# The second FFN product of 18 inner tiles by Strassen's algorithm, two tiles at a time, with running sums in DRAM

## The chip, the core and the metric

The kernel runs on one core of a Trainium2 chip. TensorE (PE in the profile) multiplies, VectorE (DVE), ScalarE (ACT) and GpSimd (POOL) do the elementwise work, and SyncE (SP) issues most DMAs; some are issued from ACT's and POOL's queues. Each engine works through its own instructions in order and waits on semaphores for the others. The metric is the device time of one execution in microseconds, the median of several runs.

## What is computed

The reference is a trunk of two residual layers over 1024 tokens of width 1024: a gated DeltaNet layer, then a chunked softmax attention layer, and a gated ConvFFN after each. The change is in the ConvFFN alone:

```python
FFN_DIM = 2816
def conv_ffn(xn, w_up, conv_w, conv_b, w_down):
    h = causal_dwconv(xn @ w_up, conv_w) + conv_b
    gate, val = h[..., :FFN_DIM], h[..., FFN_DIM:]
    return (jax.nn.silu(gate) * val) @ w_down

for layer in range(DEPTH):          # DEPTH = 2
    ...
    h = h + conv_ffn(rmsnorm(h, f_norm[layer]), f_w_up[layer], f_conv[layer], f_conv_b[layer], f_w_down[layer])
return rmsnorm(h, final_norm)
```

All data are float32. The kernel splits every matmul operand into a high and a low float32r part and adds three products (high x high, high x low, low x high). `triple` in the code is one such set of three matmuls of 128 x 128 by 128 x 512.

## The kernel before

`ffn(layer, ...)` handles one ConvFFN. The 2816 inner channels are 22 tiles of 128 (`FP = 22`). For each tile j the *first product* gives gate and val before the convolution, already by a Strassen form: seven products `product(j, n)` of 12 matmuls, n in the order 1, 7, 6, 5, 2, 4, 3, in place of eight. Their operands come from `operand(j, n)`: a VectorE sum of weight blocks where one is needed, an ACT copy for the high part (`uh`), a POOL difference for the low part (`ul`). `after(j, n)` takes results out of PSUM, mostly on VectorE (`keep`, `vpre`, `gpre`). Then come the convolution's taps (`taps`: the first on ACT, the others on VectorE over gate and val), `silu` on ACT, `gated` on VectorE, and `hidden`, which splits the 128 x 1024 tile into `hidh` (ACT) and `hidl` (VectorE).

The *second product* takes the inner tiles 0 to 17 in nine groups of two (`NG = 9`). For a group g, `down(g, u)` computes one of eight 128 x 1024 output tiles `pd` with 12 matmuls: four triples over two inner tiles and two token halves. In layer 0 outputs lie as features by tokens with the weights stationary, in layer 1 as tokens by features with the channels stationary. `down_sum` copies the result out of PSUM on ACT (`hr`) and adds it to the running sum `d_hu[u]` in DRAM by an accumulating DMA from POOL's queue; in group 0 it is written plainly from SP. In layer 0, group 0, the residual is loaded and added on VectorE; in layer 1 it comes in by transposes on PE in the steps where g = u. The last four inner tiles (18 to 21) are multiplied at the layer's end (`part`, `tile_of`), added to what is loaded back from `d_hu`, and handed on.

The order of all of this is written out by hand. `seq` lists PE's steps; a step is one `product`, one `down` or one part of the end. `at(i, f, rank)` puts other work into a list that is issued just before PE's step i, by rank. Work given at step i is not held until PE gets there: an engine goes on with its own instructions, and only a semaphore (a PSUM result, a free buffer, a landed DMA) stops it. `operand(j, n)` is given two steps ahead of its product, `after(j, n)` one step behind. From tile 3 on, a group's period is 14 products of two inner tiles and the eight `down` steps of an earlier group, placed by the offsets `offs`.

Memory is tight: all eight PSUM banks are used, four for the first product (`u`) and four for the second (`d`, two tiles of two banks), and rooms of SBUF are reused by tag. The rooms `h1_0` to `h1_7` (layer 1: `h2_0` to `h2_7`) hold the residual at the layer's start; later `hid` of three tiles in turn lies in 0 to 5, `hr` in 6 and 7.

## Time and profile before

| | |
|---|---|
| median of 3 runs | 2642.46 us (2642.02 to 2642.86) |
| profiled execution | 2643.1 us, its span 2641.4 us, granted clock 0.996 |
| PE busy | 2552.0 us, 14149 matmuls |
| VectorE, ACT, POOL busy | 1575.1, 1309.9, 1256.3 us |
| DMA moved | 303.62 MB, of it 69.21 MB on POOL's queue |
| first FFN product on PE, first to last matmul | layer 0: 681.2 to 1311.5 us; layer 1: 1946.6 to 2589.7 us |

The page of the profile gives busy times of the engines, the span in 40 slices, the DMA queues, the chain of work that ended last, the costliest groups of instructions (line, engine, operation, tiles out<-in, shape, count; then busy time, the mean of one, and the idle time before them with what ended it), and the DMA issues. Other views of the trace give the same for a stretch of time, and instructions in order of time. A stretch of 59.84 us is one period of the inner groups.

### The profile page before, as it was taken

The numbers are of one execution on the slowest core, as the hardware profiler recorded it, in microseconds if no ns is written. First come the engines' busy times: TensorE is split into PE (matmuls) and PEld (weight loads), VectorE is DVE, ScalarE is ACT, GpSimd is POOL, SyncE is SP. The second block draws the span as 40 slices with busy tenths as digits, with TensorE's granted clock in tenths as the row PEclk, the third lists the DMA queues.
The fourth block names the chain that finished last, engine by engine and source line by source line (L and its number), as shares of the span: only waits on it lengthen the run. The fifth ranks groups of instructions, "written<-read, shape, count | busy, mean of one in ns | idle before, by whom it ended". The sixth has DMA issues, their size and how long they took to land.

```text
span 2641.4 us, 39047 instructions
## 1 busy us (share of the span) xinstructions
PE 2552.0 (97%) x14149; PEld 2112.8 (80%) x14149; DVE 1575.1 (60%) x2840; ACT 1309.9 (50%) x2526; POOL 1256.3 (48%) x1330
## 2 busy tenths in 40 slices
PE   7999899999999999999999999998989999999998
PEld 5878788888778888888878788887877888888886
DVE  5755764554685555555676666666478455455556
ACT  5444456564444444444455555555345444444443
POOL 3655544345345555555535444443343455555551
PEclk9999999999999999999999999999999999999999
DMA  4434435555346666666631111114232566666654
GB/s 128 138 99 121 120 108 154 158 164 161 86 145 140 120 120 136 120 124 120 150 117 51 43 57 45 47 46 144 89 95 76 128 144 129 127 128 126 144 105 148
DMA packets 312017, 303.62 MB, mean 115 GB/s; under 512 B 32528, under 2 KB 245264, under 8 KB 311824
## 3 DMA queue, kind: packets, MB, share of 16 engines
q1 hardware_dynamic: 287856, 223.26, 28.4%
q0 software_dynamic: 19072, 69.21, 16.3%
q10 hardware_dynamic: 4896, 8.65, 0.9%
q8 instruction: 111, 1.82, 0.3%
q14 instruction: 82, 0.67, 0.1%
HBM read 183.04 MB, written 118.03 MB: 114 GB/s over the span
## 4 chain that ended last, share of the span: by engine, by line
PE 70%; DVE 8%; issue 4%; POOL 3%; DMA 2%; ACT 2%; SPq 0%; DVEq 0%; ACTq 0%; POOLq 0%
PE pu L1387 9%; PE pu L1385 9%; PE pu L1386 9%; PE acc L120 4%; PE acc L121 4%; PE acc L122 4%; PE pd L1689 2%; PE pd L1690 2%; PE pd L1688 2%; PE pd L1385 2%; PE pd L1387 2%; PE pd L1386 2%; PE acco L120 2%; PE acco L122 2%; PE acco L121 2%
## 5 line engine op out<-in xcount | busy, mean ns | idle before, releaser
L1355 POOL TENSOR_TENSOR ul<-r,uh 128x512 fp32r<-128x512 f32 x282 | 412.8, 1508 | 327.7 <-ACT uh L1373 320.2
L120 PE MATMUL acc<-xh,whi 128*128 128x512 f32 x896 | 375.2, 419 | 0.2 <-ACT xh L1094 0.2
L121 PE MATMUL acc<-xl,whi 128*128 128x512 f32 x896 | 353.7, 395 | 1.6 <-POOL xl L379 1.0
L122 PE MATMUL acc<-xh,wlo 128*128 128x512 f32 x896 | 352.9, 394 | 0.6 <-POOL wlo L105 0.6
L105 POOL TENSOR_TENSOR wlo<-wraw,whi 128x256 fp32r<-128x256 f32 (+1 forms) x293 | 235.6, 833 | 200.4 <-ACT whi L103 161.6
L1701 ACT COPY hr<-pd 128x1024 f32<-128x1024 f32 x128 | 129.9, 1015 | 311.3 <-PE pd L1690 152.6
L1373 ACT CAST uh<-r 128x512 fp32r<-128x512 f32 x296 | 180.7, 620 | 181.6 <-DVE r L1355 118.9
L1702 POOL DMA_DIRECT2D d_hu<-hr x128 | 112.1, 876 | 240.3 <-ACT hr L1701 231.2
L1387 PE MATMUL pu<-xh,ul 128*128 128x512 f32 x552 | 215.5, 390 | 5.1 <-POOL ul L1355 5.1
L1385 PE MATMUL pu<-xh,uh 128*128 128x512 f32 x552 | 215.4, 390 | 2.5 <-ACT uh L1373 1.0
L1386 PE MATMUL pu<-xl,uh 128*128 128x512 f32 x552 | 215.2, 390 | 1.0 <-POOL xl L379 1.0
L122 PEld LDWEIGHTS acc<-xh,wlo 128*128 128x128 f32 x896 | 168.9, 189 | 38.3 <-POOL wlo L105 1.0
L121 PEld LDWEIGHTS acc<-xl,whi 128*128 128x128 f32 x896 | 170.2, 190 | 25.7 <-POOL xl L379 3.1
L120 PEld LDWEIGHTS acc<-xh,whi 128*128 128x128 f32 x896 | 169.8, 190 | 22.9 <-ACT xh L1094 1.0
L1468 DVE SCALAR_TENSOR_TENSOR val<-vpre,colt,val 128x1023 f32<-128x1023 f32 (+2 forms) x92 | 115.5, 1255 | 108.8 <-ACT val L1465 108.7
L1355 DVE TENSOR_TENSOR r<-r,r 128x512 f32<-128x512 f32 x168 | 140.6, 837 | 41.6 <-POOL ul L1355 41.5
L1995 POOL TENSOR_SCALAR sS<-sS,st 128x640 f32<-128x640 f32 (+4 forms) x128 | 87.5, 687 | 141.9 <-DVE st L1994 125.2
L1355 POOL TENSOR_TENSOR dl<-dr,dh 128x512 fp32r<-128x512 f32 x72 | 121.8, 1692 | 53.8 <-ACT dh L1373 53.8
L1468 DVE SCALAR_TENSOR_TENSOR gate<-gpre,colt,gate 128x1023 f32<-128x1023 f32 (+2 forms) x92 | 145.7, 1584 | 0.3
L1355 DVE TENSOR_TENSOR keep<-pu,keep 128x512 f32<-128x512 f32 x84 | 58.0, 690 | 143.5 <-PE pu L1387 142.0
L1355 DVE TENSOR_TENSOR vpre<-pu,keep 128x512 f32<-128x512 f32 x84 | 57.7, 687 | 133.9 <-PE pu L1387 133.7
L1355 DVE TENSOR_TENSOR hidl<-val,hidh 128x1024 fp32r<-128x1024 f32 (+1 forms) x46 | 87.3, 1898 | 72.3 <-ACT hidh L1483 72.3
(376 smaller groups left out, 6820.1 us busy)
## 6 DMA issues: line engine op xcount, KB each, us to landing
d_hu<-hr POOLq DMA_DIRECT2D x128, 512.0 KB, 5.5
r<-in_f_w_up_dram SPq DMA_DIRECT2D x168, 256.0 KB, 4.9
dr<-in_f_w_down_dram SPq DMA_DIRECT2D x72, 256.0 KB, 5.2
wraw<-in_a_w_in_dram SPq DMA_DIRECT2D x32, 512.0 KB, 4.7
wraw<-in_a_w_out_dram SPq DMA_DIRECT2D x16, 512.0 KB, 3.8
d_r<-h ACTq DMA_DIRECT2D x32, 256.0 KB, 3.9
d_hu<-hr SPq DMA_DIRECT2D x16, 512.0 KB, 3.0
wraw<-in_w_kv_dram SPq DMA_DIRECT2D x16, 512.0 KB, 3.9
```

Of the source, the lines that this page charges most:

```text
L105: nc.gpsimd.tensor_tensor(lo[:, c], raw[:, c], hi[:, c].bitcast(F32), op=ALU.subtract)
L120: mm(ps, hi[:, kw, wcol : wcol + P], rh[k][s], start=st, stop=False)
L121: mm(ps, hi[:, kw, wcol : wcol + P], rl[k][s], start=False, stop=False)
L122: mm(ps, lo[:, kw, wcol : wcol + P], rh[k][s], start=False, stop=sp)
L1355: tt = lambda eng, o, a, b, op: eng.tensor_tensor(o, a, b, op=op)
L1373: copy(hi, src)
L1385: mm(ps, w[0][:, cw], x[0], start=first, stop=False, skip_group_check=True)
L1386: mm(ps, w[0][:, cw], x[1], start=False, stop=False, skip_group_check=True)
L1387: mm(ps, w[1][:, cw], x[0], start=False, stop=last, skip_group_check=True)
L1468: nc.vector.scalar_tensor_tensor(t_[:, a:c1], p_[:, a - step : c1 - step], w[:, 2 - step : 3 - step], t_[:, a:c1], op0=ALU.mult, op1=ALU.add)
L1701: nc.scalar.copy(hr, dps[g, u])
L1702: nc.gpsimd.dma_start(out=d_hu[u], in_=hr, accum_op=add)
```

## The change

The second product of the nine groups goes by Strassen's algorithm too (the form with 7 products). For two inner tiles, weights are four blocks a11, a12, a21, a22 (output half, inner tile) of 128 x 512 and channels four blocks b11 to b22 (inner tile, token half). `second(g, n)` is one of seven products of four triples, in the order 1, 2, 5, 3, 6, 7, 4, placed after every second product of the first FFN product (group 0: some after one). Its operands are prepared three steps ahead: `weights` (VectorE sums, ACT copy `dh`, POOL difference `dl`) and `channels` (sums on VectorE in place in `val`, ACT copy `eh`, difference `el` on POOL for n = 3, 6, 7, else on VectorE). `hidden` is gone for tiles 0 to 17.

Products 1 and 2 share a PSUM bank pair, 5 and 3 share one, and 6, 7 and 4 share one. `drain` takes the state out after each product: on ACT for n = 1, 2, 5, 3, 4; on VectorE for 6 and 7, which are added to what 3 and 5 left in SBUF. `send` then adds five of the seven (not 5 and 3), each as two transfers of 512 KB, to five running sums in DRAM by accumulating DMAs from POOL's queue: the first, E, is common to three output quarters, the other four belong to the quarters. In layer 0 the quarters start as the residual (`d_r`, now kept by quarters); in layer 1 they start from plain writes of group 0, and the residual comes in by transposes in the end part (`load_r`). At a layer's end E is loaded back and sent on to three quarters (`load_e`, `send_e`).

Rooms change: `val` lies in `h_0` to `h_3` in turn, the staging tiles of `drain` and of E in `h_4` to `h_7`, and `hid` of tiles 18, 19, 20 in 6 and 7, 4 and 5, 2 and 3. Weight blocks have one buffer each (`a11` to `a22`, `ay`), and rings of two hold `d` and `e`.

```diff
-        RINGS = dict(u=3, d=4 if layer == 1 else 2)
+        RINGS = dict(u=3, d=2, e=2)
...
-                    conv_t[j, v] = tp.tile([P, SEQ], F32, name=("gate", "val")[v], tag=("gate", "val")[v])
+                if v == 0:
+                    conv_t[j, v] = tp.tile([P, SEQ], F32, name="gate", tag="gate")
+                else:
+                    conv_t[j, v] = hp.tile([P, SEQ], F32, name="val", tag=f"h{layer + 1}_{j % 4}")
...
+                    room_ = {18: 6, 19: 4, 20: 2}[j]
+                    hid[j] = [hp.tile([P, SEQ], F32R, name=f"hid{i}", tag=f"h{layer + 1}_{room_ + n}") for n, i in enumerate("hl")]
...
+        ORDER = 1, 2, 5, 3, 6, 7, 4
...
-                offs = [0, 2, 3, 5, 6, 8, 9, 11]
-                if layer == 0 and g < 2:
-                    offs = ([3, 4, 6, 7, 9, 10, 12, 13], [1, 3, 4, 6, 7, 9, 10, 12])[g]
-                elif g == 0:
-                    offs = [3, 4, 5, 6, 8, 9, 10, 11]
-                for u, o in enumerate(offs):
+                for n, o in zip(ORDER, (2, 3, 5, 6, 8, 9, 11) if g == 0 else (-2, 0, 2, 4, 6, 8, 10)):
                     if c == 7 * (2 * g + 1) + 6 + o:
-                        step(("d", g, u), lambda g=g, u=u: down(g, u))
+                        step(("d", g, n), lambda g=g, n=n: second(g, n))
...
-            when[j].append((nx(j, {3: 7, 5: 6}.get(j, 5) if layer == 0 else 5), (hidden,), 1.9))
+            if j >= 2 * NG:
+                when[j].append(({18: pos["d", NG - 1, 4] + 3, 19: pos["d", NG - 1, 4] + 7}.get(j, nx(j, 5)), (hidden,), 1.9))
...
+        def weights(g, n):
+            a = lambda q: araw[g, q]
+            if n == 5:
+                araw[g, 0] = wf.tile([P, HALF], F32, name="ay", tag="ay", bufs=1)
+                tt(nc.vector, a(0), a(21), a(22), add)
+            elif n == 3:
+                tt(nc.vector, a(0), a(0), a(11), sub)
+                tt(nc.vector, a(12), a(12), a(0), sub)
+            elif n == 7:
+                tt(nc.vector, a(21), a(11), a(21), sub)
+            aops[g, n] = cut(a({1: 11, 2: 12, 5: 0, 3: 12, 6: 0, 7: 21, 4: 22}[n]), "d")
+
+        def channels(g, n):
+            b11, b12, b21, b22 = [conv_t[2 * g + k, 1][:, hs(s)] for k in range(2) for s in range(2)]
+            if n == 5:
+                tt(nc.vector, b11, b12, b11, sub)
+            elif n == 6:
+                tt(nc.vector, b11, b22, b11, sub)
+            elif n == 7:
+                tt(nc.vector, b12, b22, b12, sub)
+            elif n == 4:
+                tt(nc.vector, b21, b21, b11, sub)
+            src = {1: b11, 2: b21, 5: b11, 3: b22, 6: b11, 7: b12, 4: b21}[n]
+            bops[g, n] = cut_high(src, "e")
+            cut_low(src, *bops[g, n], nc.gpsimd if n in (3, 6, 7) else nc.vector)
+
+        def second(g, n):
+            new = n in (1, 5, 6)
+            if new:
+                banks[g] = [pacc.tile([P, SEQ], F32, name="pd", tag="d", bufs=2) for _ in range(2)]
+            w_, x_ = (aops[g, n], bops[g, n]) if layer == 0 else (bops[g, n], aops[g, n])
             for f in range(4):
+                triple(banks[g][f // 2][:, hs(f % 2)], w_, x_, kc[f], new, True)
+
+        def drain(g, n):
+            for u in range(2):
+                ps = banks[g][u]
+                if n in (6, 7):
+                    t_ = stage[g, n, u] = stage[g, 3 if n == 6 else 5, u]
+                    tt(nc.vector, t_, ps, t_, add)
+                else:
+                    t_ = stage[g, n, u] = hp.tile([P, SEQ], F32, name="stage", tag=f"h{layer + 1}_{4 + u + (0 if n in (1, 5) else 2)}")
+                    nc.scalar.copy(t_, ps)
...
+        def send(g, n):
+            for u in range(2):
+                if g == 0 and (layer == 1 or n == 1):
+                    nc.sync.dma_start(out=total(n, u), in_=stage[g, n, u])
+                else:
+                    nc.gpsimd.dma_start(out=total(n, u), in_=stage[g, n, u], accum_op=add)
+
+        def load_e(u):
+            stage["e", u] = hp.tile([P, SEQ], F32, name="stage", tag=f"h{layer + 1}_{4 + u}")
+            nc.sync.dma_start(out=stage["e", u], in_=d_e[u])
+
+        def send_e(n):
+            for u in range(2):
+                nc.gpsimd.dma_start(out=total(n, u), in_=stage["e", u], accum_op=add)
...
+            for q, n in ((11, 7), (12, 3), (21, 7), (22, 4)):
+                at(b_[n] - 2, lambda g=g, q=q: load_a(g, q), 3 + q / 100)
+            for n in ORDER:
+                at(p_[n] - 3, lambda g=g, n=n: weights(g, n), 1.2)
+                at(p_[n] - 3, lambda g=g, n=n: channels(g, n), 1.4)
+                at(p_[n] + 1, lambda g=g, n=n: drain(g, n), 0)
+                if n not in (3, 5):
+                    at(p_[n] + 2, lambda g=g, n=n: send(g, n), 0.5)
+        fin_at = pos["d", NG - 1, 4]
+        for u in range(2):
+            at(pos["d", NG - 1, 7] + 3, lambda u=u: load_e(u), 3)
+        for n, i in ((6, 4), (7, 5), (4, 6)):
+            at(fin_at + i, lambda n=n: send_e(n), 0.5)
```

Here `b_` is the step of product n in the group before. The removed functions (`down`, `down_sum`, `load_dn`, `load_row`, `load_h`, `load_r` of the groups) and the changed addresses of the loads at a layer's end are left out.

More of the change, by code (lines that the diff above doesn't have):

```diff
@@ L497, in trunk_kernel @@
     ctx_h = ExitStack()
-    d_r0, d_r1 = [[dram.tile([P, SEQ], F32, name=f"d_r{i}_{k}") for k in range(KT)] for i in range(2)]
+    d_r0, d_r1 = [{(c, s, u): dram.tile([P, SEQ], F32, name=f"d_r{i}_{c}{s}{u}") for c in range(2) for s in range(2) for u in range(2)} for i in range(2)]
+    quarter = lambda d, m, s: d[m // 4, s, m % 4 // 2][:, hs(m % 2)]
     d_y = [[dram.tile([P, HALF], F32, name=f"d_y{k}_{s}") for s in range(2)] for k in range(KT)]
@@ L1355, in ffn @@
         tt = lambda eng, o, a, b, op: eng.tensor_tensor(o, a, b, op=op)
-        d_hu = [dram.tile([P, SEQ], F32, name=f"d_hu{layer}_{u}") for u in range(KT)]
+        d_c = d_r if layer == 0 else {x_: dram.tile([P, SEQ], F32, name=f"d_c{x_[0]}{x_[1]}{x_[2]}") for x_ in d_r}
+        d_e = [dram.tile([P, SEQ], F32, name=f"d_e{layer}_{u}") for u in range(2)]
         left, right = ExitStack(), ExitStack()
@@ L1692, in down_sum @@
-        def down_sum(g, u):
-            hr = hrs[g, u]
-            if g == 0 and layer == 0:
-                tt(nc.vector, hr, dps[g, u], hr, add)
-                nc.sync.dma_start(out=d_hu[u], in_=hr)
-            elif g == 0:
-                nc.scalar.copy(hr, dps[g, u])
-                nc.sync.dma_start(out=d_hu[u], in_=hr)
-            else:
-                nc.scalar.copy(hr, dps[g, u])
-                nc.gpsimd.dma_start(out=d_hu[u], in_=hr, accum_op=add)
-        past, free = [], 0
@@ L1802, in fin_h @@
                     for m in range(KT):
[L1803 removed]
+                        nc.sync.dma_start(out=fh[m][:, hs(s)], in_=quarter(d_c, m, s))
                 rooms = [x for _ in range(3) for x in ("uh", "ul")]
@@ L1819, in load_t, with load_r @@
                 for c in range(2):
-                    nc.sync.dma_start(out=fh[t][:, hs(c)], in_=d_hu[4 * c + t // 2][:, hs(t % 2)])
+                    nc.sync.dma_start(out=fh[t][:, hs(c)], in_=d_c[c, t // 4, t % 4 // 2][:, hs(t % 2)])
+            res = {}
+            def load_r(t):
+                for c in range(2):
+                    if t < 4:
+                        tag = ("eh", "el", "dh", "dl")[t % 2 * 2 + c]
+                        r_ = wf.tile([P, 4, P], F32, name="res", tag=tag, bufs=2)
+                    else:
+                        r_ = actp.tile([P, 4, P], F32, name="res", tag=f"x{'hl'[c]}{t}_1")
+                    for u in range(2):
+                        nc.sync.dma_start(out=r_[:, 2 * u : 2 * u + 2], in_=d_r[c, t // 4, u].rearrange("p (f t) -> p f t", f=2)[:, :, kc[t % 4]])
+                    res[t, c] = r_
             def tile_of(t, ks):
@@ L1830, in f @@
                     for c in range(2):
+                        if ks[0] == 0:
+                            for f in range(4):
+                                nc.tensor.matmul(fps[t][c][:, f * P : (f + 1) * P], res[t, c][:, f], ident, is_transpose=True, start=f == 0, stop=False, skip_group_check=True)
                         for k in ks:
```

100 lines of the change are left out of this document (25 added, 75 removed).

## The prediction, on record before the changed kernel was run

> **What bounds the kernel now.** I read the page's engine shares first, then the stretches of 59.84 us that one group of the second FFN product takes, then the groups of instructions, the order in time on VectorE and POOL, and last the DMA queues.
>
> ```profile
> span 2641.4 us, 39047 instructions
> PE 2552.0 (97%) x14149; PEld 2112.8 (80%) x14149; DVE 1575.1 (60%) x2840; ACT 1309.9 (50%) x2526; POOL 1256.3 (48%) x1330
> ```
>
> A busy PE is not yet a PE at its pace, so the stage matters. Next come two groups of layer 0: all instructions, then those of the second product (`pd`), then those of the first (`pu`).
>
> ```profile
> 881.00:940.84 59.84, 59.84 (x266) 49.57 (x265) 34.73 (x32) 28.56 (x38) 32.68 (x28) 1.00 0.66 128
> 940.84:1000.68 59.84, 59.84 (x266) 49.56 (x265) 32.27 (x31) 28.55 (x38) 32.61 (x27) 1.00 0.64 123
> ```
>
> ```profile
> 940.84:1000.68 59.84, 23.06 (x98) 18.02 (x97) 0.00 (x0) 8.12 (x8) 1.00 0.64 123
> ```
>
> ```profile
> 940.84:1000.68 59.84, 39.38 (x168) 31.54 (x168) 6.89 (x10) 2.32 (x4) 1.00 0.64 123
> ```
>
> The columns are PE, its weight load, VectorE, ACT and POOL, then the granted clock, DMA share and GB/s (the last two rows lack POOL). PE never stops at a granted clock of 1.00. A group is 14 products of 12 matmuls for the first FFN product and 8 tiles of 12 for the second, 264 in all (266 with those that cross an edge). So 59.84/266 = 0.225 us for each matmul, and 22 steps of 2.72 us. The mean of 389 ns in the groups is longer since matmuls overlap, and it is not the price. In this stage the time is the number of matmuls; the other engines stand at 32.3, 28.6 and 32.6 of 59.84.
>
> **The change, part by part.** The durations, of six groups of layer 0:
>
> ```profile
> L1355 POOL TENSOR_TENSOR ul<-r,uh 128x512 fp32r<-128x512 f32 x85 | 122.5, 1490 | 62.5 <-ACT uh L1373 62.5
> L1373 ACT CAST uh<-r 128x512 fp32r<-128x512 f32 x84 | 51.5, 620 | 48.0 <-DVE r L1355 32.1 <-issue 15.6
> L1701 ACT COPY hr<-pd 128x1024 f32<-128x1024 f32 x48 | 48.7, 1015 | 105.4 <-PE pd L1387 104.8
> L1702 POOL DMA_DIRECT2D d_hu<-hr x48 | 42.0, 874 | 78.5 <-ACT hr L1701 71.2 <-ACT uh L1373 7.1 <-issue 0.2
> L1355 DVE TENSOR_TENSOR val<-val,gate 128x1024 f32<-128x1024 f32 x12 | 22.8, 1898 | 0.0
> L1355 DVE TENSOR_TENSOR hidl<-val,hidh 128x1024 fp32r<-128x1024 f32 x12 | 21.7, 1806 | 19.7 <-ACT hidh L1483 19.7
> L1355 DVE TENSOR_TENSOR keep<-pu,keep 128x512 f32<-128x512 f32 x24 | 16.6, 692 | 43.5 <-PE pu L1387 43.1
> L1468 DVE SCALAR_TENSOR_TENSOR val<-vpre,colt,val 128x1023 f32<-128x1023 f32 x12 | 15.4, 1284 | 33.5 <-ACT val L1465 33.5
> L1483 ACT CAST hidh<-val 128x1024 fp32r<-128x1024 f32 x12 | 12.6, 1052 | 0.0
> ```
>
> How VectorE and POOL hold each other up, in order of time:
>
> ```profile
> 966.52 0.68 DVE L1355 TENSOR_TENSOR r<-r,r 128x512 f32<-128x512 f32 x1
> 967.12 1.28 DVE L1468 SCALAR_TENSOR_TENSOR val<-vpre,colt,val 128x1022 f32<-128x1022 f32 x1
> 969.58 0.69 DVE L1355 TENSOR_TENSOR r<-r,r 128x512 f32<-128x512 f32 x1 [1.18 <-POOL ul L1355]
> 970.19 2.31 DVE L1468 SCALAR_TENSOR_TENSOR gate<-gpre,colt,gate 128x1023 f32<-128x1023 f32 x1
> ...
> 974.69 1.27 DVE L1468 SCALAR_TENSOR_TENSOR gate<-gpre,colt,gate 128x1022 f32<-128x1022 f32 x1
> ```
>
> ```profile
> 970.11 1.31 POOL L1355 TENSOR_TENSOR dl<-dr,dh 128x512 fp32r<-128x512 f32 x1 [0.57 <-ACT dh L1373]
> ```
>
> *PE.* Seven products of 12 replace eight tiles of 12: 12 matmuls less in each of 9 groups of 2 layers, 216 x 0.225 = 48.6 us off the engine that sets the end. The period would be 59.84 - 2.70 = 57.1 us. The residual's 64 transposes in layer 1 move to the end, equal in number: nothing either way.
>
> *VectorE, per group.* Two `hidl` go (-3.6 us). Four sums of channels, four of weights and four `el` come, 512 wide, and four drains (n = 6, 7) of 1024 out of PSUM: 12 x 0.68 (the undisturbed `r<-r,r`) + 4 x 1.38 (two `keep`) = 13.7. So 32.3 + 10.1 = 42 of 57.1.
>
> *ACT.* Out go two `hidh`, four `dh` and eight drains (2.1 + 2.5 + 8.1), in come fourteen copies of 512 and ten drains (8.7 + 10.2): +6.2, 35 of 57.1.
>
> *POOL.* Four `dl` become seven, three `el` are new, and eight accumulating DMAs become ten: 6 x 1.49 + 2 x 0.87 = +10.7, 43 of 57.1.
>
> No engine is above PE by its sum. What decides is lateness: an operand is made two steps (5.44 us) ahead, by a VectorE sum, an ACT copy and a POOL difference (0.68 + 0.62 + 1.49 = 2.8). VectorE is gated by PE wherever it reads PSUM. Its fullest stretch goes from the drain of n = 6 to the next `keep`, five steps or 13.6 us. In it the new order has two drains (5.5), a `gpre`, two tile sums, a channel sum and an `el` (5 x 0.68), another tile sum (0.68) and four taps (5.1): 14.7 by the rows, but adjacent VectorE rows overlap by about 0.09 (966.52 + 0.68 against 967.12), so some 13.5. VectorE thus falls two to three us behind there, the 2.6 us of slack are used up, and it catches up in the next five steps, where it has some 6 us of work. POOL's fullest three steps hold four differences (6.0) of 8.2. I take 0.2 us of stall for each of 16 inner groups, +3; the ends are 0 and the rival on the interface below.
>
> *The interface that VectorE and POOL share.* The tap at 970.19 starts inside POOL's difference (970.11 to 971.42) and takes 2.31 instead of 1.27: it waits most of that difference. The Trainium skill, "SBUF — State Buffer", section "Who interferes with whom", says that a VectorE instruction with two SBUF inputs and a POOL instruction that reads SBUF exclude each other for the whole instruction. The trace agrees, by that 1.04 us. What it would make of the time is the third rival.
>
> *SP's and POOL's queues, inside the groups.* Loads of second-product weights stay four per group of 256 KB each; the eight residual loads and eight plain writes of layer 0's first group go. Each new load waits for the last reader of its only buffer, a difference of the step before, so SP stands up to 2 us; behind it are loads of up-weights that are needed more than five steps later: nothing. POOL's sends of n = 6 and 7 wait for VectorE's drain, and the next `ul` stands behind them; that is in the two to three us of lateness above.
>
> *The start of each layer.* Without `hidden` for tiles 0 to 2 the head gets lighter on VectorE, and group 0's operands, with one product instead of two between some of its seven, make it heavier. I take 0, with 3 us either way per layer.
>
> *The tail, where the DMAs come in.*
>
> ```profile
> q1 hardware_dynamic: 287856, 223.26, 28.4%
> q0 software_dynamic: 19072, 69.21, 16.3%
> ...
> d_hu<-hr POOLq DMA_DIRECT2D x128, 512.0 KB, 5.5
> r<-in_f_w_up_dram SPq DMA_DIRECT2D x168, 256.0 KB, 4.9
> ```
>
> An accumulating transfer of 512 KB lands 5.5 us after issue. Queue 0 spends 16.3% of 2641.4 us on 69.21 MB, 3.26 us of all sixteen engines for each 0.524 MB, so transfers issued close together land 3.26 apart. Inside a group that is covered: ten take 33 of 57 us, and a staging tile is written again only four or five steps (11 to 14 us) after its send. At a layer's end it is not. Put 0 at PE's start of the last product (n = 4, group 8). It ends at 2.7, ACT has drained it at 4.9, and POOL sends its two halves at 6.5 behind one `ul`. Then come six more, the first sum E added to three totals (`send_e`, indices +4 to +6). Eight transfers one behind another: the last lands at 6.5 + 5.5 + 7 x 3.26 = 34.8. Now `hidden(19)`, at index +7 (19.0 us), writes into the rooms `h_4` and `h_5` that E was staged in. ACT waits for the seventh, VectorE for the eighth, and all that is queued behind waits too: the difference ends at 36.6, a gate tap at 37.9, `keep` and `keep7` at 39.2. The last tile's product 4 adds onto the bank that `keep7` reads. It would start at index +10, 27.2, so PE stands 12 us, and about 1 more for product 3, whose sum is queued behind `gated`. `hidden(18)` waits likewise for its two sends, within the lead. SP waits for E's last accumulation before it loads E back, with the last tile's two loads behind it, needed five and more steps later; POOL's `ul` of products 7, 6 and 5 stand between the six sends and are ready by their step or an us late, inside the 12. That is 13 per layer, +26. The low end: if each lands 5.5 after its own issue (about 22 for the last) VectorE is through at 32, +9 for both layers. The high end: loads run ahead of them (0.88 us of queue 1 for each 256 KB, 28.4% of the span over 223.26 MB): eight last weight tiles, 7 us a layer, and in layer 1 sixteen residual pieces, 7 more, +47. I take the middle: most weight loads fall in gaps before.
>
> *Sum.* -48.6 + 3 + 0 + 26 = -19.6. The profiled execution took 2643.1, 0.6 above the median of 2642.46 of the three runs: 2643.1 - 19.6 = 2623.5, against the median 2623.
>
> **The rivals.** *The tail is hidden.* The sends keep pace and the inner groups lose nothing: -48.6 + 9 = 2603. For it: a single send lands in 5.5 with loads beside it. Against: six go out in about three steps, which this trace never has.
>
> *The tail eats it.* Loads in front, +47: -48.6 + 3 + 47, 2644, no change.
>
> *Slower: VectorE and POOL run out of their shared interface, in the inner groups.* Per group POOL has 24 differences of 1.31, VectorE 20 instructions of 0.68 and 10 of 1.28 with two SBUF inputs: 31.4 + 13.6 + 12.8 = 57.8 of 57.1, where before it was 18 x 1.31 + 8 x 0.68 + 12 x 1.28 = 44.4 of 59.84. If nothing overlaps, the interface and not PE sets the pace; filled to 95%, a group takes 60.8 and 18 of them lose 63 us against the forecast's 57.3: 2686. It decides from a period of 58.4 us, where 18 x 1.1 us use up the 19.6. Against it: a POOL row lasts 1.31 and the tap lost 1.04, so about 0.2 of each difference is free of it, 24 x 0.2 = 5 us per group, and some 53 of 57 remain. The page named above, whose rule holds the interface for the whole instruction, would make it this rival.
>
> That PE's count does not fall is no rival: the loops fix 84 for 96.
>
> **How the numbers follow.** Forecast 0.44 (2610 to 2637), tail hidden 0.18, tail eats it 0.14, interface 0.24. What a measurement can tell from no change is 0.2%, 5.3 us. Faster gets the forecast and the hidden tail, 0.62; same gets most of the third, 0.13; slower the interface and a rest, 0.25. The range of 8 in 10 goes from 2600 to 2664: from just below the hidden tail into the milder half of the interface case.
>
> **What would show it.** Right: windows of 57.1 us with about 254 matmuls and PE full; POOL near 43, VectorE 42 to 46 in them; ten accumulating sends per group; one PE gap of some 12 us per layer before the last tile's product 4, released by VectorE's `keep`, with ACT's `hidh` waiting for a DMA. Wrong: gaps in every group, with `ul` or `dl` as releaser and VectorE taps of over 2 us (third rival), or no such gap at the ends (first).

## The result: slower by 1.57%

| | median, us | range, us | ratio to before |
|---|---|---|---|
| before | 2642.24 (4 runs) | 2641.02 to 2642.86 | 1 |
| after | 2683.79 (4 runs) | 2680.91 to 2685.69 | 1.0157, 95% 1.0139 to 1.0175 |

The forecast was 2623, its range 2600 to 2664. The page of the changed kernel:

```profile
span 2683.3 us, 39404 instructions
...
PE 2542.1 (95%) x13933; PEld 2083.7 (78%) x13933; DVE 1807.4 (67%) x3084; ACT 1410.3 (53%) x2714; POOL 1492.2 (56%) x1490
```

PE has its 216 matmuls less (14149 to 13933), yet the span is 41.9 us longer. To find the places, I take two marks in each layer from the view of a tile's instructions: the product with `x7` (product 7 of the first FFN product, once per inner tile) and the product with `x` and `uh`, whose last start is nearly the end of the first product. Each row ends with its first and its last start. Before:

```profile
L1385 PE MATMUL pu<-x7h,uh x84: 389/389/497, 717.6 to 1296.2; 128*128 128x512 f32 x84
...
L1385 PE MATMUL pu<-xh,uh x276: 387/389/486, 681.2 to 1311.0; 128*128 128x512 f32 x138
...
L1385 PE MATMUL pu<-x7h,uh x84: 389/389/389, 1986.4 to 2571.1; 128*128 128x512 f32 x84
...
L1385 PE MATMUL pu<-xh,uh x276: 387/389/501, 1946.6 to 2589.3; 128*128 128x512 f32 x138
```

After:

```profile
L1389 PE MATMUL pu<-x7h,uh x84: 389/389/794, 728.1 to 1304.5; 128*128 128x512 f32 x84
...
L1389 PE MATMUL pu<-xh,uh x276: 387/389/794, 685.8 to 1329.4; 128*128 128x512 f32 x138
...
L1389 PE MATMUL pu<-x7h,uh x84: 389/389/793, 2019.3 to 2594.4; 128*128 128x512 f32 x84
...
L1389 PE MATMUL pu<-xh,uh x276: 389/389/794, 1977.6 to 2624.1; 128*128 128x512 f32 x138
```

| stretch, us | before | after | change |
|---|---|---|---|
| start of the span to layer 0's first `x7` | 717.6 | 728.1 | +10.5 |
| layer 0, first to last `x7` | 578.6 | 576.4 | -2.2 |
| layer 0, last `x7` to last `x` | 14.8 | 24.9 | +10.1 |
| to layer 1's first `x7` | 675.4 | 689.9 | +14.5 |
| layer 1, first to last `x7` | 584.7 | 575.1 | -9.6 |
| layer 1, last `x7` to last `x` | 18.2 | 29.7 | +11.5 |
| to the end | 52.1 | 59.2 | +7.1 |

The sum is +41.9. The layer starts lose 25 us where the forecast had none. The ends lose 21.6 where it had 26. The long middle gains 11.8 where 216 matmuls are worth 48.6. (The last row and 7 us of the layer 1 middle belong together: the residual's 64 transposes went from the groups to the end.)

**The middle.** One group by engine (columns as in the prediction: PE, weight load, VectorE, ACT, POOL, clock, DMA share, GB/s), and the change's fixed point in each group, the sum `ay<-ay,a` that occurs once, in layer 0:

```profile
951.40:1009.80 58.40, 57.71 (x254) 47.06 (x253) 45.46 (x45) 33.58 (x49) 45.19 (x35) 1.00 0.71 143
```

```profile
L1357 DVE TENSOR_TENSOR ay<-ay,a x7: 677/677/680, 898.9 to 1249.3; 128x512 f32<-128x512 f32 x7
```

254 matmuls, as forecast, but the period is (1249.3 - 898.9) / 6 = 58.40 and not 57.1 to 57.3. VectorE (45.5) and POOL (45.2) are near what I summed (42 to 46, and 43). Of PE's lost 1.3 us, 1.0 stands at one place, product 3 of the second FFN product. PE, VectorE and POOL in order of time there:

```profile
963.41 0.50 PE L1390 MATMUL pd<-el,dh 128*128 128x512 f32 x1 [0.69 <-POOL el L1357]
```

```profile
955.63 1.77 DVE L1357 TENSOR_TENSOR r<-r,r 128x512 f32<-128x512 f32 x1
...
958.64 2.32 DVE L1475 SCALAR_TENSOR_TENSOR gate<-gpre,colt,gate 128x1022 f32<-128x1022 f32 x1
```

```profile
958.18 1.70 POOL L1357 TENSOR_TENSOR ul<-r,uh 128x512 fp32r<-128x512 f32 x1 [1.34 <-ACT uh L1377]
959.84 2.28 POOL L1357 TENSOR_TENSOR dl<-a,dh 128x512 fp32r<-128x512 f32 x1
962.08 1.28 POOL L1357 TENSOR_TENSOR el<-val,eh 128x512 fp32r<-128x512 f32 x1
```

VectorE has no idle time in this stretch and POOL none from 958.18 on; a tap and a weights' low half side by side take 2.32 and 2.28 us, where each alone takes 1.27 to 1.30. `el`, which PE waits for, is third in POOL's queue.

**The first groups.** The same 410 matmuls, in tiles 3 to 6 of layer 0, before and after:

```profile
753.20:846.30 93.10, 93.04 (x410) 76.42 (x409) 60.03 (x58) 39.68 (x54) 45.53 (x32) 1.00 0.57 154
```

```profile
763.90:865.60 101.70, 95.86 (x410) 75.61 (x409) 81.23 (x76) 59.86 (x84) 71.63 (x54) 1.00 0.59 126
```

Here group 0 costs 8.6 us: VectorE goes from 60 to 81 us and POOL from 46 to 72, in about as much time. Layer 1 has the same waits: between 2060 and 2108 us seven matmuls start 0.4 to 1.05 us late, some 5 us in all.

**The layer starts.** The view of who waited for whom shows a wait of the first up-weight loads that is new (window 655 to 700, after):

```profile
DVE rsn L373 <- ACT rsn L372: 13.7, 1, 13.7
POOL r L1435 <- DVE nacc L364: 8.1, 1, 8.1
...
ACT uh L1377 <- DMA r<-in_f_w_up_dram: 7.0, 1, 7.0
```

POOL's loads of the raw up-weights (`r`) wait 8.1 us for the norm's running sum `nacc`; SP's wait 18.8. So they land late, ACT's copy `uh` waits 7.0 for them, and PE waits 5.7 and 2.8 us for the operands made from them. The norm's own sum on PE (`pss`) stands behind these matmuls, ACT's `rsn` waits for it, and VectorE waits 13.7 us for `rsn` (3.2 before). In layer 1 POOL waits 11.6 us in the same way.

**The ends.** The last tile of layer 0, in order of time:

```profile
1314.56 1.04 ACT L1492 CAST hidh<-val 128x1024 fp32r<-128x1024 f32 x1 [6.30 <-DMA d_r<-stage]
1317.44 1.23 DVE L1357 TENSOR_TENSOR hidl<-val,hidh 128x1024 fp32r<-128x1024 f32 x1 [6.65 <-DMA d_r<-stage]
...
1319.77 1.41 DVE L1357 TENSOR_TENSOR keep<-pu,keep 128x512 f32<-128x512 f32 x2
...
1321.57 0.79 PE L1389 MATMUL pu<-xt4h,uh 128*128 128x512 f32 x1 [7.19 <-ACT uh L1377]
```

That is the forecast's gap: ACT, then VectorE, wait for the staging transfers, `keep` comes behind them, and PE stands 7.2 us before product 4. The last thing that PE waits for is ACT's `uh`, some 0.3 us behind `keep`. In layer 1 the gaps there are 6.8 and 1.9 us. Just ahead of these stretches, before the last tile's `x7`, PE stands 3.54 us in layer 0 and 4.26 in layer 1.

**The granted clock.** Its mean over the span is 0.981 in the changed kernel and 0.996 before. In the inner groups it is 1.00 in both, so it has no part in their 1.3 us. At the starts and the ends it has. The stretch from 660 to 700 us, before and after:

```profile
660.00:700.00 40.00, 37.62 (x179) 30.74 (x178) 17.77 (x25) 12.82 (x21) 23.60 (x26) 1.00 0.49 139
```

```profile
660.00:700.00 40.00, 31.48 (x131) 25.32 (x131) 6.40 (x11) 5.91 (x9) 17.00 (x21) 0.83 0.47 137
```

From the last `x7` to the last `x` it falls from 1.00 to 0.76 in layer 0 and from 1.00 to 0.79 in layer 1. Where it is 0.50, matmuls start 0.42 us apart in place of 0.23. Counted over both traces, 104 matmuls do so in the changed kernel and 21 before, so some 16 of the 41.9 us (an estimate, 0.2 us each) are PE at the lower clock behind the waits told above.

### The profile page after: what moved, and what is told of

Read it like the earlier page. It is cut to its first block, busy times and chain, and to the rows that moved or that the text cites. A ratio compares the mean times of both kernels' runs of the same rounds, so it can differ in the third digit from the quotient of the medians.

```text
span 2683.3 us, 39404 instructions
## 1 busy us (share of the span) xinstructions
PE 2542.1 (95%) x13933; PEld 2083.7 (78%) x13933; DVE 1807.4 (67%) x3084; ACT 1410.3 (53%) x2714; POOL 1492.2 (56%) x1490
## 4 chain that ended last, share of the span: by engine, by line
PE 40%; issue 8%; DVE 8%; POOL 7%; ACT 3%; DMA 3%; ACTq 0%; DVEq 0%; POOLq 0%
PE pu L1391 5%; PE pu L1390 4%; PE pu L1389 4%; PE acc L120 3%; PE acc L121 3%; POOL ul L1357 3%; PE acc L122 3%; PE pd L1391 2%; PE pd L1390 2%; PE pd L1389 2%; DVE r L1357 2%; DVE val L1475 2%; PE ptp L2047 2%; PE poT L2077 1%; ACT uh L1377 1%
## 5 line engine op out<-in xcount | busy, mean ns | idle before, releaser
L1357 POOL TENSOR_TENSOR ul<-r,uh 128x512 fp32r<-128x512 f32 x282 | 440.2, 1571 | 354.4 <-ACT uh L1377 331.7
L1357 DVE TENSOR_TENSOR r<-r,r 128x512 f32<-128x512 f32 x168 | 178.0, 1059 | 19.2 <-POOL ul L1357 19.1
L1475 DVE SCALAR_TENSOR_TENSOR val<-vpre,colt,val 128x1023 f32<-128x1023 f32 (+2 forms) x92 | 154.3, 1677 | 39.3 <-ACT val L1472 39.2
L1695 ACT COPY stage<-pd 128x1024 f32<-128x1024 f32 x180 | 173.2, 1012 | 1.1 <-PE pd L1391 1.0
L1357 POOL TENSOR_TENSOR dl<-a,dh 128x512 fp32r<-128x512 f32 x90 | 160.5, 1784 | 20.5 <-ACT dh L1377 20.5
L1389 PEld LDWEIGHTS pu<-xh,uh 128*128 128x128 f32 x552 | 105.7, 191 | 49.9 <-POOL uh L1377 18.1
L1475 DVE SCALAR_TENSOR_TENSOR gate<-gpre,colt,gate 128x1023 f32<-128x1023 f32 (+2 forms) x92 | 134.4, 1461 | 0.2
L2025 ACT ACTIVATE sS<-sS,st 128x640 f32<-128x640 f32 (+4 forms) x128 | 89.1, 696 | 83.2 <-DVE st L2024 83.0
L1391 PEld LDWEIGHTS pu<-xh,ul 128*128 128x128 f32 x552 | 105.5, 191 | 33.3 <-POOL ul L1357 11.4
L1357 DVE TENSOR_TENSOR el<-val,eh 128x512 fp32r<-128x512 f32 x72 | 68.0, 945 | 90.5 <-ACT eh L1377 90.5
```

What stands on the lines that cost most here:

```text
L1357: tt = lambda eng, o, a, b, op: eng.tensor_tensor(o, a, b, op=op)
L1389: mm(ps, w[0][:, cw], x[0], start=first, stop=False, skip_group_check=True)
L1391: mm(ps, w[1][:, cw], x[0], start=False, stop=last, skip_group_check=True)
L1475: nc.vector.scalar_tensor_tensor(t_[:, a:c1], p_[:, a - step : c1 - step], w[:, 2 - step : 3 - step], t_[:, a:c1], op0=ALU.mult, op1=ALU.add)
L1695: nc.scalar.copy(t_, ps)
L2025: nc.scalar.activation(S, S, AF.Exp, bias=st[:, 1:2], accum_out=st[:, 2:3])
```

## The experiments

The period below is that of `ay<-ay,a` in layer 0, its six distances between 860 and 1260 us. Each ratio is to the kernel before, run on the same chip; e1 to e4 shared a chip, e5 to e11 another, e12 and e13 a third, and e14 ran on a fourth. e7, e8 and e12 leave work out and are there for their times alone.

| run | ratio | 95% | period, us |
|---|---|---|---|
| e1 rooms moved | 1.0057 | 1.0042 to 1.0072 | 58.38 |
| e2 and the sum's rooms | 1.0005 | 0.9996 to 1.0014 | 58.38 |
| e3 one operand early (from the changed kernel) | 1.0197 | 1.0180 to 1.0214 | 59.42 |
| e4 all of these | 1.0059 | 1.0042 to 1.0076 | 59.42 |
| e5 base: e2, two copies moved | 0.9992 | 0.9982 to 1.0001 | 58.38 |
| e6 base, one low half on VectorE | 1.0040 | 1.0025 to 1.0055 | 59.32 |
| e7 base, two far low halves left out | 0.9941 | 0.9921 to 0.9961 | 57.73 |
| e8 base, a tap left out | 0.9919 | 0.9900 to 0.9939 | 57.23 |
| e9 base, the tap later | 0.9979 | 0.9969 to 0.9988 | 58.00 |
| e10 e9, groups put off | 1.0097 | 1.0081 to 1.0113 | 59.83 |
| e11 the kernel before, padded | 1.0037 | 1.0023 to 1.0050 | |
| e12 base, one-input operation for the tap | 0.9964 | 0.9949 to 0.9979 | 57.85 |
| e13 e9, sigmoid later | 0.9967 | 0.9956 to 0.9979 | 57.92 |
| e14 e13, sends spread | 0.9933 | 0.9917 to 0.9950 | 57.93 |

**The layer starts: e1 and e11.** The weight pool `wf` lies at the right end of memory, its rooms in the order in which tags are first asked for. The change made it larger, so the rooms of the first up-weights slid to other addresses.

```diff
+        for x, n in ((("a11", 1), ("a12", 1), ("ay", 1), ("eh", 2)) if layer == 0 else (("ay", 1),)):
+            wf.tile([P, HALF], F32, name=x, tag=x, bufs=n)
         late = [room(1, q) for q in (21, 22)]
```

> The changed kernel with its tiles asked for in another order in the FFN's weight pool and nothing else: a few tiles are asked for ahead of the first up-weight rooms, so that these rooms lie at the addresses that they had in the kernel before in layer 0, and off the norm's buffers in layer 1. Theory (rooms): the changed kernel's first up-weight loads wait for the norm because their rooms now lie where the norm still computes; the layer starts then come back by 10.5 us in layer 0 and 15.0 us in layer 1, some 25 us, about 2658 us, and the wait of the first loads for the norm's tile (8.1 us on POOL, 18.8 us on SP in layer 0) is gone. If group 0 was late only because the start was, up to 9 us more, 2650. Rival (drift or clock): the start was late because of what lies before it or of a lower granted clock; the loads go out earlier and the time stays within 5 us of 2684. The period of the inner groups stays at 58.4 us by both.

```profile
L1389 PE MATMUL pu<-x7h,uh x84: 389/389/628, 716.9 to 1293.0; 128*128 128x512 f32 x84
...
L1389 PE MATMUL pu<-xh,uh x276: 387/389/628, 680.5 to 1318.3; 128*128 128x512 f32 x138
...
L1389 PE MATMUL pu<-x7h,uh x84: 389/389/793, 1993.1 to 2568.1; 128*128 128x512 f32 x84
...
L1389 PE MATMUL pu<-xh,uh x276: 389/389/794, 1952.8 to 2597.6; 128*128 128x512 f32 x138
```

Layer 0's first `x7` is at 716.9 (728.1 in the changed kernel), and the way from layer 0's last `x` to layer 1's first `x7` is 674.8 (689.9): 11.2 + 15.1 = 26.3 us, for 25.5 expected, with not one operation changed. By the ratios it is 1.0% or 26 us. e11 turns it round: the kernel before with 8 KB that nobody uses.

```diff
+        if layer == 0:
+            wf.tile([P, 8 * 256], F32, name="pad", tag="pad", bufs=1)
         def cut0(r, c):
```

> The kernel before with one unused tile of 8 KB in each partition at the end of layer 0's weight pool, which moves the rooms of the first up-weights to lower addresses; nothing else. Theory (rooms): the first loads of layer 0 now wait for the norm as in the changed kernel, and the time rises by some 10.5 us, about 1.004 times the kernel before. Rival (rooms do not matter, the start was late for another reason): within 0.1% of the kernel before.

```profile
DVE rsn L373 <- ACT rsn L372: 14.1, 1, 14.1
POOL r L1431 <- DVE nacc L364: 9.0, 1, 9.0
```

The same two waits appear (9.0 and 14.1), and the kernel before gets 0.37% slower, 9.8 us, where 10.5 were expected. Rooms alone make and unmake this loss in layer 0; for layer 1 there is e1 alone. The granted clock follows: from 660 to 700 us it is 1.00 in e1 and 0.83 in e11.

**The ends: e2, e5 and e14.** e2 keeps e1's rooms and stages the first product's sum in half tiles in rooms of its own:

```diff
-            stage["e", u] = hp.tile([P, SEQ], F32, name="stage", tag=f"h{layer + 1}_{4 + u}")
-            nc.sync.dma_start(out=stage["e", u], in_=d_e[u])
+            stage["e", u] = [wf.tile([P, HALF], F32, name="es", tag=x, bufs=1) for x in (("a21", "ay"), ("a22", "se"))[u]]
+            for s in range(2):
+                nc.sync.dma_start(out=stage["e", u][s], in_=d_e[u][:, hs(s)])
...
-                nc.gpsimd.dma_start(out=total(n, u), in_=stage["e", u], accum_op=add)
+                for s in range(2):
+                    nc.gpsimd.dma_start(out=total(n, u)[:, hs(s)], in_=stage["e", u][s], accum_op=add)
```

> As the run with the moved rooms, and the last additions of the first product's sum staged in four rooms of their own (half tiles) instead of the two rooms that the hidden tile of inner tile 19 needs next; 12 half sends instead of 6 whole ones at a layer's end. Theory (tail): tile 19's hidden copy waits only for these transfers; without them the ends lose most of the 12.6 and 13.9 us that they cost, all but the 3.5 us that tile 18's copy holds up, some 20 us in all: 20 us below the run with the moved rooms, about 2638. Rival (the transfers themselves, or the end part's loads behind them, bind): it stays within 6 us of the run with the moved rooms, or is slower for the 6 more sends per layer.

```profile
L1389 PE MATMUL pu<-x7h,uh x84: 389/389/628, 715.8 to 1290.7; 128*128 128x512 f32 x84
...
L1389 PE MATMUL pu<-xh,uh x276: 387/389/628, 678.1 to 1309.4; 128*128 128x512 f32 x138
...
L1389 PE MATMUL pu<-x7h,uh x84: 389/389/797, 1984.2 to 2557.7; 128*128 128x512 f32 x84
...
L1389 PE MATMUL pu<-xh,uh x276: 387/389/504, 1944.2 to 2580.7; 128*128 128x512 f32 x138
```

From a layer's first `x7` to its last `x` e1 takes 601.4 and 604.5, e2 593.6 and 596.5: 15.8 us back, 0.52% by the ratios, against 20 expected. The theory holds; that the extra sends take the rest was not tested. e5 also lets the two hidden copies follow the landing of the sends from their rooms:

```diff
-{18: pos["d", NG - 1, 4] + 3, 19: pos["d", NG - 1, 4] + 7}
+{18: pos["d", NG - 1, 4] + 5, 19: pos["d", NG - 1, 4] + 2}
```

> The moved rooms, the first product's sum in rooms of its own, and tile 19's and tile 18's hidden copies moved behind the landing of the sends from their rooms; product 3's operand where the changed kernel has it. It is the base for the three others. Theory (the last gap of 3.5 us at an end is tile 18's copy): 5 us below the run with rooms and tail, about 2638, inner period 58.4 us. Rival: no difference to that run.

It is 0.13% below e2, some 3 us, with intervals that overlap, so the 5 us are not shown; in its profile the gaps of 3.5 and 4.3 us before the last tile's `x7` are gone. What is left at the ends of e5 shows in POOL's order there:

```profile
1283.12 3.53 POOL L1722 DMA_DIRECT2D d_r<-es  x4
1285.36 3.47 POOL L1357 TENSOR_TENSOR ul<-r,uh 128x512 fp32r<-128x512 f32 x1
1286.60 5.73 POOL L1722 DMA_DIRECT2D d_r<-es  x4
1290.35 3.48 POOL L1357 TENSOR_TENSOR ul<-r,uh 128x512 fp32r<-128x512 f32 x1
```

Four sends take POOL up to 5.7 us, and each `ul` that PE needs stands among them and takes 3.5 us where others take 1.3 to 2. e14 (on e13, below) spreads them:

```diff
-        for n, i in ((6, 4), (7, 5), (4, 6)):
-            at(fin_at + i, lambda n=n: send_e(n), 0.5)
+        for i, (n, u) in enumerate([(n, u) for n in (6, 7, 4) for u in range(2)]):
+            at(fin_at + 4 + i, lambda n=n, u=u: send_e(n, u), 2)
```

> The run with the sigmoid later, and the twelve half sends of the first product's sum at a layer's end in six steps, two behind each step's up-weight low half, instead of three steps with four ahead of it. Theory (POOL's issue: four sends hold POOL some 5 us, and the up-weight low half queued behind them is what PE waits for, 1.0, 1.9 and 1.7 us at the last tile's products in layer 0): these waits go, 3 to 5 us per layer, 2625 to 2629. Rival (the sends' landing binds the end part's loads, which now come later): no gain, or up to 5 us slower.

The ratio is 0.34% below e13's, some 9 us; the intervals just fail to meet (0.9950 and 0.9956), on two chips. In the profiles PE's waits for `ul` before the last tile's first products are gone, but in layer 0 waits of 0.9, 1.2 and 1.7 us stand at later products instead; from first `x7` to last `x` layer 0 gains 1.6 us and layer 1 6.2. The rival shows too: in layer 0's end part SP's loads of `h` wait 10.4 us in all for these sends (in e13 not at all), and PE waits 3.62 us for `h` where it waits 0.56 in e13. That the one makes the other is read from the order and not tested. The two profiled spans, 2628.8 and 2629.7 us, are nearly the same. So the theory is half right: POOL's issue time has to go somewhere, and the sends land later.

**The inner groups: e3, e6 to e10, e12, e13.** Two theories stood: one POOL operand in the wrong place, or a shared interface of VectorE and POOL that is full.

```diff
-                at(p_[n] - 3, lambda g=g, n=n: channels(g, n), 1.4)
+                at(p_[n] - (4 if n == 3 else 3), lambda g=g, n=n: channels(g, n), 1.4)
```

> The changed kernel with one edit: the channel operand of product 3 of the second product is cut one step earlier, so that its low half stands ahead of the weights' low half in POOL's queue. Theory (one late operand): the 1.29 us by which an inner group is over its 57.12 us is PE waiting for that one POOL operand; the period falls from 58.4 to about 57.4, some 16 us over 16 inner groups, about 2668. Rival (VectorE and POOL run out of the shared interface): POOL's operations are late because they share with VectorE, another operand is late in its place, the period stays within 0.3 us of 58.4 and the time within 5 us of 2684.

```profile
L1357 DVE TENSOR_TENSOR ay<-ay,a x7: 1776/1781/1782, 900.8 to 1257.3; 128x512 f32<-128x512 f32 x7
```

Both missed the period, which rose to 59.42, though another operand is late in `el`'s place, as the rival had it. The early `el` now runs beside VectorE's sum `ay`, which takes 1.78 us in every group instead of 0.68; PE no longer waits for `el`, but for `ul`, three times in each group. e4 had e3's edit with e1's, e2's and e5's:

> All three edits, and at the layers' ends tile 19's hidden copy five steps and tile 18's two steps moved so that each follows the landing of the sends from its rooms. If the three theories hold and their gains add: 25 + 20 + 16 + some 5 for the last gap, about 2618, faster than the kernel before by about 0.9%. If the shared interface is what binds the inner groups, about 2634; if the layer starts do not come back, about 2643.

1.0059; e3's edit costs it what it cost alone. e6 gives that low half to VectorE, behind the tap:

```diff
-            cut_low(src, *bops[g, n], nc.gpsimd if n in (3, 6, 7) else nc.vector)
+            if n != 3:
+                cut_low(src, *bops[g, n], nc.gpsimd if n in (6, 7) else nc.vector)
...
+                if n == 3:
+                    at(p_[n] - 3, lambda g=g: cut_low(conv_t[2 * g + 1, 1][:, hs(1)], *bops[g, 3], nc.vector), 2.05)
```

> The base with product 3's low half of the channels made by VectorE, behind that step's tap, instead of POOL. Theory (place: POOL has one difference too many between its operands for products of the first FFN product there): POOL's queue is shorter by 1.3 us at the one place where it is late, the period falls to 57.2 to 57.6 and the time by 13 to 19 us, about 2622. Rival (rate: the shared interface is full over the whole group): VectorE's 0.7 us in place of POOL's 1.3 takes at most 0.6 us off the period, 57.8 or more, the gain is under 10 us. Rival (VectorE is late there instead): period 58.4 or more.

59.32, the last of the three: VectorE has no room either. Then two runs that leave work out. e7 drops two POOL low halves far from the stall (`aops[g, n] = hi, hi` for n = 1, 4 and g > 0), e8 drops the gate's third tap (`g2` out of the step `nx(j, 3)`) of every tile, two in a group:

> The base with two of POOL's seven weight low halves left out in the inner groups, those of products 1 and 4, which lie 20 us and more from the place of the stall (the matmuls read the high half twice, so the work of PE is the same). Theory (place): the stall at product 3 stays as it is, period 58.3 to 58.4. Rival (rate): the interface has 2 x 1.3 us less to do in each group, the period falls by as much as PE allows, to 57.1 to 57.3.

> The base with the gate's third tap left out in all inner tiles (VectorE's operation that stands in the trace beside the late weights' low half: 2.32 us for it and 2.28 us for the low half, each alone 1.28). Theory (place, and POOL is late there because it shares with that tap): the low half takes about 1.3 us, product 3's operand is 1 us earlier, the period falls to 57.1 to 57.5. Rival (place, POOL's queue alone is too long, shared or not): the period stays within 0.3 us of 58.4. By the rate theory it falls too, so this run does not speak on that.

e7: 57.73, where the place theory had 58.4 and the rate theory 57.1 to 57.3: half a cure, from 20 us away. e8: 57.23, the whole cure (252 matmuls of 0.227 us take 57.2), from two taps in a group, one beside POOL ahead of product 3 (2.32 us) and one some 30 us later (1.27). Which of the two counts, it can't say. e9 moves the first of them, the even tile's, into VectorE's idle time:

```diff
+            if j % 2 == 0 and j < FP - 2:
+                when[j][3:] = [(nx(j, 5), (g2, silu), 2), (nx(j, 6), (gated,), 2)]
```

> The base with the gate's third tap and the sigmoid of each even inner tile two products later, and its product with the gate three products later: they move from the stretch where VectorE has no idle time (some 13 us up to product 2 of the first FFN product) into the 3.8 us in which it waits for PE behind it. No operation is left out or added. Theory (place: VectorE and POOL fall behind in one stretch of the group): period 57.2 to 57.5, as with the tap left out, some 20 us over 18 groups, about 2621. Rival (rate: the interface is full over the whole group): the period stays at 58.2 to 58.4, about 2640. Rival (the tap collides with the next drains): above 58.4.

58.00, a third of what leaving out both taps gives, and no theory's number; at its new place that tap takes 2.31 us again. It does make the kernel faster than before, by 0.21%. e10 moves all groups against the taps:

```diff
-for n, o in zip(ORDER, (2, 3, 5, 6, 8, 9, 11) if g == 0 else (-2, 0, 2, 4, 6, 8, 10)):
+for n, o in zip(ORDER, (2, 4, 6, 8, 10, 12, 13) if g == 0 else (0, 2, 4, 6, 8, 10, 12)):
```

> As the run before, and the second product's places put off: group 0 at every second product from its first on instead of two products of the second kind with one between, and all later groups two products later. Theory (group 0 is slow, 10 us in layer 0, because its seven products come closer than VectorE and POOL make their operands): a further 5 to 8 us in layer 0, 0 to 4 in layer 1, about 2613. Rival (the head is slow for the taps and sums of the first tiles, not for group 0): within 3 us of the run before. Rival (the last transfers now land later): the ends lose up to 10 us.

```profile
L1357 DVE TENSOR_TENSOR ay<-ay,a x7: 3221/3270/3273, 898.5 to 1257.5; 128x512 f32<-128x512 f32 x7
```

A miss: 59.83. The same sum of 0.68 us now takes 3.27 in every group, beside two of POOL's `ul`. A shift of two products between the two streams of work costs 1.8 us per group, so e10 can't say whether the wider spacing helped group 0. e12 separates the interface from VectorE's time, with an operation of one SBUF input in the place of each of e8's taps:

```diff
+        def reduce_(j):
+            t_ = tp.tile([P, 1], F32, name="top", tag="top")
+            nc.vector.tensor_reduce(t_, conv_t[j, 0], axis=AX.X, op=ALU.max)
...
-(nx(j, 3), (g2, silu), 2)
+(nx(j, 3), (reduce_, silu), 2)
```

> The base with the gate's third tap replaced, in the same place of VectorE's order, by an operation of about the same length with one input in SBUF instead of two (the maximum of the gate tile along its row, 1024 elements into one; the tap itself is left out, so its own work is missing in the output). Theory (the shared interface: the tap costs the inner groups by keeping POOL out): the period is that of the run with the tap left out, 57.2 to 57.5, and POOL's low half beside it takes 1.3 us instead of 2.28. Rival (VectorE's time: the tap costs by keeping VectorE's next sums back): the period stays at 58.2 to 58.4. In between: both.

VectorE and POOL of e12 at the place of the stall:

```profile
1008.55 1.21 DVE L1479 TENSOR_REDUCE top<-gate 128x1 f32<-128x1024 f32 x1
```

```profile
1008.10 1.69 POOL L1357 TENSOR_TENSOR ul<-r,uh 128x512 fp32r<-128x512 f32 x1 [1.34 <-ACT uh L1377]
1009.76 1.29 POOL L1357 TENSOR_TENSOR dl<-a,dh 128x512 fp32r<-128x512 f32 x1
```

VectorE's operation lies wholly beside `ul`, as the tap's first half did, but takes 1.21 us (the tap 2.32), and `dl` behind it takes 1.29 (2.28). The period is 57.85: of the 1.15 us that the two taps cost a group, 0.53 come from sharing with POOL and 0.62 from VectorE's plain time. The second can be more, since in e8 PE is at its pace and no period can fall further. The Trainium skill, "SBUF — State Buffer", section "Who interferes with whom", says that a VectorE instruction with at most one SBUF input, outside certain modes, does not contend with POOL, and one with two does where POOL reads SBUF; these rows agree. Last, e13 puts the sigmoid of odd tiles behind ACT's next copies:

```diff
+            if j % 2 and j < FP - 2:
+                when[j][3:] = [(nx(j, 3), (g2,), 2), (nx(j, 4), (silu, gated), 2)]
```

> The run with the even tiles' tap later, and the sigmoid of each odd inner tile put behind the next copies on ACT instead of ahead of them: in the run before it waits for its tap, and the copy behind it reaches POOL so late that PE stands 0.65 us before product 5 in each group. Theory (order on ACT): that gap goes, the period falls from 58.0 to 57.3 to 57.5, 9 to 12 us, about 2627. Rival (the whole of POOL and VectorE is full): the gap moves to another product, period 57.8 to 58.0.

57.92, the rival's number: PE still waits some 0.5 us for an `ul` in each group. Moves shifted the gap and gave back 0.46 us of 1.15 at best; only less work took it away.

**What this leaves.** Of the runs that do all of the change's work e14 is the fastest, 0.67% faster than the kernel before. Its groups still take 0.6 us more than the forecast's 57.3.

## Why the prediction was wrong, step by step

- *PE, -48.6: right.* 216 matmuls fewer, 254 in a group's window.
- *The layer starts, 0 with 3 either way: wrong, some +25.* I looked only at VectorE's work there. The step that failed is that the first up-weight loads on SP's and POOL's queues were put at nothing, with no look at the addresses of their rooms: they wait for the norm, 8.1 us on POOL in layer 0 and 11.6 in layer 1. e1 and e11 show the cause. The trace of before could have warned only in part (it has no such wait on POOL); the pool's size in the diff could have.
- *The inner groups, +3: wrong in size, 16 x 1.28 = +20.* The failed step is "I take 0.2 us". I had found VectorE's fullest stretch as 13.5 us of work in 13.6, with undisturbed rows of 0.68, and then let 2.6 us of slack absorb it. In the trace after, such sums take up to 1.77 beside POOL, and the place is the stretch ahead of product 3, not the one behind the drain of n = 6. The same lines are the signs named for the third rival, a gap in every group and taps over 2 us, with `el` as releaser in place of `ul` or `dl`.
- *The shared interface as a rival: half the mechanism, and the wrong size.* It priced 60.8 us per group; measured were 58.4, and e12 gives sharing about half of what two taps cost. That its 2686 lies near 2684 is chance: 25 of the 42 us came from the starts.
- *Group 0: wrong, +8.6 in layer 0 and some 5 in layer 1.* "Heavier" was seen and then netted to 0. No run tested it by itself; the engine sums above fit the cause found for the inner groups, which is an argument and not a proof.
- *The tail, 13 per layer: right in mechanism and nearly in size.* The last `x7` to the last `x` lost 10.1 and 11.5, with the named waits; PE also stood 3.5 and 4.3 us just ahead of that stretch, for tile 18's copy, which I had called within the lead. In place of a gap of 12 us there was one of 7.2 with slower matmuls behind it (last section).
- *The clock: no term.* The sum takes a granted clock of 1.00 throughout. Behind the new waits it is 0.50, some 16 us in all, which are part of the losses above and not beside them.
- *The sum of it.* The span grew by 41.9 us where PE's work fell by 48.6, so 90.5 us were lost: 25 at the starts, 21.6 at the ends, 20 in the inner groups, 13.6 in the first groups and 7.8 before the last `x7`. Some 2 us are not accounted for.
- *"That PE's count does not fall is no rival"* stands. A rival that I lacked was a loss in instructions that the change does not touch.

## What to carry to other kernels

When a change makes a pool larger or smaller, ask what its first tiles now lie upon: a load that waits for the last reader of old bytes can cost 10 us a stage, and asking for the tags in another order brings it back. Where VectorE and POOL are both near 80% of a period, count some 1 us more for a VectorE operation with two SBUF inputs that starts beside POOL (here 0.68 took 1.77 and 1.27 took 2.32), and take work away rather than move it: two moves of one operation here cost a group some 1 us each, and a third gained 0.4 us. At a stage's end, give transfers that are staged last rooms that nobody needs next, and count POOL's issue time for each against the operands behind it.

## What was not expected of the hardware

A short gap of PE has a long shadow. In the changed kernel PE stood 3.54 us before the last tile's `x7` in layer 0:

```profile
1300.02 0.79 PE L1389 MATMUL pu<-x7h,uh 128*128 128x512 f32 x1 [3.54 <-ACT uh L1377]
...
1305.38 0.63 PE L1391 MATMUL pu<-x7h,ul 128*128 128x512 f32 x1
1305.81 0.59 PE L1389 MATMUL pu<-xt2h,uh 128*128 128x512 f32 x1
1306.23 0.39 PE L1390 MATMUL pu<-xt2l,uh 128*128 128x512 f32 x1
1306.47 0.40 PE L1391 MATMUL pu<-xt2h,ul 128*128 128x512 f32 x1
```

For 5.8 us behind it matmuls start 0.42 apart, then 0.23: some 3 us more than the gap itself. The granted clock is 0.50 from 1299.4 to 1306.2 us. In e5 a gap of 2.40 us in layer 1, after four of 0.6 to 2.0 within 17 us, had the same effect:

```profile
2573.98 0.80 PE L1389 MATMUL pu<-xt4h,uh 128*128 128x512 f32 x1 [2.40 <-ACT uh L1377]
...
2578.48 0.63 PE L1389 MATMUL pu<-xt4h,uh 128*128 128x512 f32 x1
2578.91 0.63 PE L1390 MATMUL pu<-xt4l,uh 128*128 128x512 f32 x1
```

The Trainium skill, "TensorE: Matmul & The Clock Gate", section "Why this matters for your kernels", asks for no idle gaps above some 3 us. The first gap agrees; the second is below that and was followed by the slow pace all the same, at a clock of 0.50. Nor does the last gap alone decide: in the first tiles of layer 0 PE waits 1.73 us for the same `ul` in both kernels, before at 738.5 us with a clock of 1.00 behind it, and in the changed kernel at 749.0 with 0.51 from 749.8 to 753.2. What else decides is open.

Accumulating transfers of 512 KB took 7.6 to 9.3 us to land in the changed kernel, where single ones took 5.5 before:

```profile
d_r<-stage POOLq DMA_DIRECT2D x78, 512.0 KB, 7.6
d_c<-stage POOLq DMA_DIRECT2D x70, 512.0 KB, 8.0
...
d_e<-stage POOLq DMA_DIRECT2D x32, 512.0 KB, 9.3
```

They go out in pairs now. The prediction had 3.26 us for each further one behind the first; the difference of 2.1 to 3.8 is of that size, but no run separates the pairs from the rest of the traffic.
